# A transformer layer's down projection by seven products of half-size blocks

## The chip, the core and the metric

The kernel runs on one core of a Trainium2 chip. A core has a matrix engine (TensorE, PE in the rows; its weight loads are PEld), VectorE (DVE), ScalarE (ACT), GpSimd (POOL), and SyncE (SP), whose queue issues all the transfers between the chip's main memory and the on-chip memory SBUF. TensorE adds up its results in eight banks of a second memory, PSUM. The metric is the device time of one execution in microseconds (us). Every engine takes its instructions strictly in the order of its own queue and waits for the others by semaphores.

## The reference

One layer on 1024 tokens of width 1024: two mixers, merged and projected, then a SwiGLU network with 2816 hidden channels and a gated embedding. The change lies in the third line below and in what leads to and from it.

```python
x = x + merged @ w_out
hf = rms_norm(x, norm_ffn_g)
x = x + (jax.nn.silu(hf @ w_ffn_gate) * (hf @ w_ffn_up)) @ w_ffn_down
hp = rms_norm(x, norm_ple_g)
x = x + jax.nn.sigmoid(hp @ w_ple_gate) * (p @ w_ple_proj)
```

## The kernel before

Everything is held transposed: channels lie on the 128 partitions, the 1024 tokens on the free axis, in two halves of 512 (`hv(t, h)`). Each float32 operand is split into two parts of a shorter format: `split_to` lets ScalarE cast it to hi (line 1046) and VectorE subtract to lo (line 1047), `split_scaled` does it in lines 171 and 174. One product of blocks is then three matmuls of 128x128 by 128x512, hi by hi, hi by lo and lo by hi (`mm3`, lines 154 to 156).

**Gate and up** (lines 1156 to 1184) run over 22 values of f, one for each 128 hidden channels. This stage already computes the two pairs of half-size products by seven products instead of eight, each of 12 matmuls (`block`). For that, `ffn_weights(f + 1)`, called in the middle of f, forms four differences of the weights: two on GpSimd (lines 1132 and 1133) and two on VectorE (1134, which needs the result of 1133, and 1135). The blocks alternate between PSUM's tags z and m, three banks each; line 1161 copies the second block's bank (s1, the bank that line 1169 reads again) and VectorE adds the others (lines 1163, 1166, 1169, 1173, 1175, 1180). GpSimd also does lines 1176 and 1179 (twice). The hidden channels c11 and u4 (one for each half of the tokens) are stored in main memory, `hid` (line 1184), and SP fetches the weights of f + 2 in lines 1124 and 1126.

**The down projection** (lines 1241 to 1268) runs over two halves of the output channels and 22 values of f. In each of the 44 steps it loads half of the weights' tile (256 KB, line 1216) and one tile of hidden (512 KB, line 1219), splits both, and does 24 matmuls into eight banks: four blocks of output channels by two halves of tokens. The first two steps use buffers that exist before this stage. After 22 steps VectorE adds the eight banks to x1, the layer's x so far, which is loaded from `x1d` (line 1259), and `residual_norm` prepares the operands of the last stage. That last stage multiplies by `w_ple_gate`.

The order of TensorE's work is that of the program text (`manual_schedule`). On the other engines a scheduler of the language sets the order by its own estimates when the kernel is built; it may put an instruction far ahead of its place in the text if its inputs and its buffer are free.

Of the kernel before, what the change touches and what calls it, by code (L numbers as in the profile page):

```python
# [9 lines left out]
F32 = mybir.dt.float32  # L10
R = mybir.dt.float32r
# [3 lines left out]
ALU = mybir.AluOpType  # L15
# [4 lines left out]
P = 128  # L20
T = 1024
# [4 lines left out]
NFF = D_FF // P  # L26
HG_HEADS = 4
# [35 lines left out]
def layer(ctx, tc, xT, pT, wts, wf_in, consts, masks, outT):  # L63
# [37 lines left out]
    def wide(tag, dt, bufs=None):  # L101
        return wpool.tile([P, WIDE], dt, tag=tag, bufs=bufs, name=tag)
# [43 lines left out]
    def weight(u, ahead=2):  # L146
        for i in range(pos[u], min(pos[u] + ahead + 1, len(order))):
            if (order[i] < U_GATE) == (u < U_GATE):
                prep(order[i])
        return splits.pop(u)  # L150

    def mm3(ps, w, x, k, first, last):

        mm(ps, w[0], x[0], start=first, stop=False)  # L154
        mm(ps, w[0], x[1], start=False, stop=False)  # L155
        mm(ps, w[1], x[0], start=False, stop=last)  # L156
# [959 lines left out]
    hid = dram.tile([D_FF, T], F32, name="hid")  # L1116
    w6 = lambda: bp.tile([P, HALF], F32, tag="w6", name="w6")
    w7 = lambda: ap.tile([P, HALF], F32, tag="w7", bufs=4, name="w7")
# [36 lines left out]
    bp = astack.enter_context(tc.tile_pool(name="bp", bufs=8, reuse_waits="tile"))  # L1155
    for f in range(NFF):
# [26 lines left out]
        for h, s in ((0, c11), (1, u4)):  # L1183
            dma(hid[f * P:(f + 1) * P, h * HALF:(h + 1) * HALF], s)
# [5 lines left out]

    x1p = ctx.enter_context(tc.tile_pool(name="x1p", bufs=8, side="right", reuse_waits="tile"))
    dq = ctx.enter_context(tc.tile_pool(name="dq", bufs=4, reuse_waits="tile"))
    dp = ctx.enter_context(tc.tile_pool(name="dp", bufs=3, reuse_waits="tile"))
    hp = [[], []]
    x1 = []
    acc = const.tile([P, T], F32, tag="rb", name="acc")

    def residual_norm(j, h, t):
        hp[h].append(split_scaled(t, sm[:, S_PLE + j:S_PLE + j + 1], h))
        if j == 0:  # L1200
            act(hv(acc, h), t, AF.Square)
        else:
            sq = dp.tile([P, HALF], F32, tag="o", bufs=4, name="sq")
            act(sq, t, AF.Square)
            ptt(hv(acc, h), hv(acc, h), sq, ALU.add)  # L1205

    def down_operands(half, f):
        if half == 0 and f < 2:
            raw = hv(wide("raw", F32, 2)[:, 0:D], 0)
            hi = hv(wide("whi", R)[:, 0:D], 0)  # L1210
            lo = hv(wide("wlo", R)[:, 0:D], 0)
        else:
            raw = dp.tile([P, HALF], F32, tag="dr", name="dr")
            hi = dp.tile([P, HALF], R, tag="dhi", name="dhi")
            lo = dp.tile([P, HALF], R, tag="dlo", name="dlo")
        dma(raw, wts[U_DOWN + f][:, half * HALF:(half + 1) * HALF])
        w = split_to(raw, None, hi, lo)
        raw = wide("raw", F32, 2)[:, 0:D]
        dma(raw, hid[f * P:(f + 1) * P, :])
        return w, [split_scaled(hv(raw, h), None, h) for h in range(2)]  # L1220
# [15 lines left out]
    def down_order():  # L1236
        for half in range(2):
            for f in (range(NFF) if half == 0 else range(NFF - 1, -1, -1)):
                yield half, f

    todo = list(down_order())
    ready = [down_operands(*todo[i]) for i in range(2)]
    for n, (half, f) in enumerate(todo):
        w, a = ready.pop(0)
        first, last = n % NFF == 0, n % NFF == NFF - 1
        if first:
            banks = [[abank(), abank()], [zbank(), zbank()], [zbank(), mbank()], [mbank(), mbank()]]
        if n + 2 < len(todo):
            ready.append(down_operands(*todo[n + 2]))
        if n == NFF + 4:  # L1250
            ple_operands()
        for jj in range(4):
            s = slice(jj * P, (jj + 1) * P)
            for h in range(2):
                mm3(banks[jj][h], (w[0][:, s], w[1][:, s]), a[h], f, first, last)
        if first:
            for jj in range(4):
                t = x1p.tile([P, T], F32, tag="x1", name="x1")
                dma(t, x1d[(half * 4 + jj) * P:(half * 4 + jj + 1) * P, :])
                x1.append(t)  # L1260
        if last:
            for jj in range(4):
                for h in range(2):
                    t = hv(x1[half * 4 + jj], h)
                    tt(t, banks[jj][h], t, ALU.add)
            for jj in range(4):
                for h in range(2):
                    residual_norm(half * 4 + jj, h, hv(x1[half * 4 + jj], h))
# [10 lines left out]
    def gate_products(w, bank, h, ks):  # L1279
        for k in ks:  # L1280
            s = slice(k * P, (k + 1) * P)
            mm3(bank, (w[0][:, s], w[1][:, s]), hp[h][k], k, k == 0, k == KT - 1)
# [101 lines left out]
```

## Time and profile before

| | us |
|---|---|
| median of three runs | 1667.92 (1667.17 to 1668.07) |
| the profiled execution | 1666.99 |
| its span, first to last instruction | 1665.2 |
| gate and up, about | 883.6 to 1302.7 |
| down projection, about | 1302.7 to 1547.6 |

The profile is of one execution. Its views are a page with the busy shares, groups of instructions by line, a timeline, and tables by stretches of time. A row names the line of the kernel, the engine, the operation, what it writes and reads (buffer numbers left out), the shape, and in square brackets how long the engine was idle before it and whose work ended that.

### The profile page before, as it was taken

Reading aid. Unit: us, or ns where it says so; the run is one execution under the profiler, and the core shown is the slowest. Engines: PE = TensorE matmul, PEld = TensorE weight load, DVE = VectorE, ACT = ScalarE, POOL = GpSimd, SP = SyncE. Lnnn points to the kernel's source line nnn. Section 1 sums busy time; section 2 is a strip of 40 time slices with the busy share of each in tenths; the row PEclk is TensorE's granted clock in tenths of the full one; section 3 lists DMA queues with packets and bytes.
Section 4 is the critical chain, followed back from the end, with each engine's and each line's share of the span. In section 5 each row is a group of like instructions: output and inputs, shape, how many; then the busy total and the mean of one; then the engine's idle time right before and its main releaser. Section 6 shows DMA issues by size and latency. Waiting matters only on the chain. (4 is left out here: it accounts for less than half of the span.)

```text
span 1665.2 us, 21335 instructions
## 1 busy us (share of the span) xinstructions
PE 1639.5 (98%) x8218; PEld 1375.5 (83%) x8218; DVE 1041.2 (63%) x1466; ACT 634.4 (38%) x943; POOL 455.1 (27%) x364
## 2 busy tenths in 40 slices
PE   8999999999999999999999999999999999999998
PEld 6889889999797777778888888888888788788887
DVE  8357778755666676565677776666777442643542
ACT  7244655642423134551344333333333342543310
POOL 2342444531313021122234444344343000200300
PEclk9999999999999999999999999999999999999999
DMA  5323121236263632361433222222221663354020
GB/s 209 102 86 105 64 77 39 77 105 189 84 158 109 183 94 85 114 228 51 152 139 102 76 77 96 94 76 76 76 89 65 243 230 114 121 201 140 26 76 38
DMA packets 93685, 185.94 MB, mean 112 GB/s; under 512 B 11376, under 2 KB 40432, under 8 KB 93584
## 3 DMA queue, kind: packets, MB, share of 16 engines
q1 hardware_dynamic: 93584, 184.59, 33.9%
q8 instruction: 64, 1.05, 0.3%
q14 instruction: 37, 0.30, 0.1%
HBM read 130.95 MB, written 40.96 MB: 103 GB/s over the span
## 5 line engine op out<-in xcount | busy, mean ns | idle before, releaser
L154 PE MATMUL ps_z<-xhi,whi 128*128 128x512 f32 x630 | 255.1, 405 | 1.4 <-DVE w L1175 0.6
L155 PE MATMUL ps_z<-xlo,whi 128*128 128x512 f32 x630 | 246.5, 391 | 0.8 <-DVE xlo L174 0.5
L156 PE MATMUL ps_z<-xhi,wlo 128*128 128x512 f32 x630 | 246.0, 390 | 0.0
L154 PEld LDWEIGHTS ps_z<-xhi,whi 128*128 128x128 f32 x630 | 119.4, 190 | 23.5 <-DVE w L1175 1.1
L156 PEld LDWEIGHTS ps_z<-xhi,wlo 128*128 128x128 f32 x630 | 118.3, 188 | 24.8
L155 PEld LDWEIGHTS ps_z<-xlo,whi 128*128 128x128 f32 x630 | 118.8, 189 | 23.4 <-DVE xlo L174 2.0
L127 ACT CAST whi<-raw 128x1024 fp32r<-128x1024 f32 (+1 forms) x69 | 72.4, 1049 | 163.9 <-PE ps_z L155 126.6
L128 DVE TENSOR_TENSOR wlo<-raw,whi 128x1024 fp32r<-128x1024 f32 (+1 forms) x69 | 99.3, 1440 | 35.3 <-ACT whi L127 24.4
L174 DVE TENSOR_TENSOR xlo<-raw,xhi 128x512 fp32r<-128x512 f32 x88 | 58.7, 689 | 92.4 <-ACT xhi L171 82.1
L400 PE MATMUL ps_z<-whi,xhi 128*128 128x256 f32 (+1 forms) x384 | 112.8, 294 | 0.0
L401 PE MATMUL ps_z<-wlo,xhi 128*128 128x256 f32 (+1 forms) x384 | 108.7, 283 | 0.0
L402 PE MATMUL ps_z<-whi,xlo 128*128 128x256 f32 (+1 forms) x384 | 108.5, 283 | 0.0
L888 POOL TENSOR_SCALAR ph<-p 128x512 fp32r<-128x512 f32 (+3 forms) x96 | 53.5, 562 | 169.9 <-ACT p L884 169.5
L1179 POOL TENSOR_TENSOR w<-w,rb 128x512 f32<-128x512 f32 x44 | 62.8, 1428 | 114.1 <-ACT w L1178 114.1
L171 ACT ACTIVATE xhi<-raw 128x512 fp32r<-128x512 f32 x88 | 52.8, 626 | 104.6 <-PE ps_m L155 57.7
L889 DVE TENSOR_TENSOR pl<-p,ph 128x512 fp32r<-128x512 f32 (+3 forms) x96 | 55.9, 590 | 49.2 <-POOL ph L888 48.8
L1205 POOL TENSOR_TENSOR acc<-acc,sq 128x512 f32<-128x512 f32 x14 | 22.2, 1617 | 227.3 <-issue 116.6
L401 PEld LDWEIGHTS ps_z<-wlo,xhi 128*128 128x128 f32 x384 | 73.3, 191 | 0.7
L400 PEld LDWEIGHTS ps_z<-whi,xhi 128*128 128x128 f32 x384 | 73.4, 191 | 0.1
L402 PEld LDWEIGHTS ps_z<-whi,xlo 128*128 128x128 f32 x384 | 73.0, 190 | 0.0
L884 ACT ACTIVATE p<-ps_m 128x512 f32<-128x512 f32 (+3 forms) x96 | 46.2, 491 | 70.2 <-PE ps_m L880 46.9
L1134 DVE TENSOR_TENSOR rg<-ru,rg 128x512 f32<-128x512 f32 x22 | 36.7, 1667 | 55.4 <-POOL ru L1133 55.4
(465 smaller groups left out, 4380.8 us busy)
## 6 DMA issues: line engine op xcount, KB each, us to landing
raw<-wts SPq DMA_DIRECT2D x71, 512.0 KB
raw<-hid SPq DMA_DIRECT2D x44, 512.0 KB
rg<-wts SPq DMA_DIRECT2D x22, 512.0 KB
ru<-wts SPq DMA_DIRECT2D x22, 512.0 KB
hid<-w SPq DMA_DIRECT2D x44, 256.0 KB
dr<-wts SPq DMA_DIRECT2D x42, 256.0 KB
gd<-gst SPq DMA_DIRECT2D x24, 256.0 KB
g<-gd SPq DMA_DIRECT2D x24, 256.0 KB
```

The costliest lines, as they stand in the source:

```text
L127: nc.scalar.copy(hi, raw)
L128: tt(lo, raw, hi.bitcast(F32), ALU.subtract)
L154: mm(ps, w[0], x[0], start=first, stop=False)
L155: mm(ps, w[0], x[1], start=False, stop=False)
L156: mm(ps, w[1], x[0], start=False, stop=last)
L174: tt(lo, src, hi.bitcast(F32), ALU.subtract)
L400: mm(ps[:, off:off + n], xh[:, cs], hi, start=k == 0, stop=False)
L401: mm(ps[:, off:off + n], xh[:, cs], lo, start=False, stop=False)
L402: mm(ps[:, off:off + n], xl[:, cs], hi, start=False, stop=k == KT - 1)
L888: pts(ph[:, 0:n], p[:, 0:n], 1.0, 0.0, ALU.mult, ALU.add)
L889: tt(pl[:, 0:n], p[:, 0:n], fb(ph[:, 0:n]), ALU.subtract)
L1179: ptt(s, s, hv(rb, h), ALU.mult)
```

## The change

The down projection, too, is done by seven products of half-size blocks. The hidden channels are taken in 11 pairs of f (kp): the two tiles of a pair and the two halves of the tokens give four blocks, the pair's weights and the two halves of the output channels give four more. For each pair there are seven hidden operands (B11, B21, B22 as they are, T1 to T4 differences) and seven weight operands (three as they are, S1 to S4 sums). All of one product's 11 pairs are done before the next product begins, in 77 steps of 12 matmuls into four banks; a bank is added to the output blocks that contain its product (the lists in `products`), some while it goes on accumulating.

The sums are formed during gate and up: `down_sums` loads a quarter of a pair's weights into the tile sw, of which there is one, GpSimd does four operations 256 wide, and the result is stored to `sd`. `store_hidden` and the lines before it do the differences of the hidden channels on GpSimd and store the operands to `hb`. A step of the down projection loads two pieces of 256 KB into one tile (now four buffers) and splits them together. All eight x1 tiles are loaded early in the stage, and the first two gate products of the last stage are put in another order.

```diff
+NPAIR = NFF // 2
...
-    def mm3(ps, w, x, k, first, last):
-        mm(ps, w[0], x[0], start=first, stop=False)
-        mm(ps, w[0], x[1], start=False, stop=False)
-        mm(ps, w[1], x[0], start=False, stop=last)
+    def mm3(ps, w, x, k, first, last, more=False):
+        mm(ps, w[0], x[0], start=first, stop=False, skip_group_check=more)
+        mm(ps, w[0], x[1], start=False, stop=False, skip_group_check=more)
+        mm(ps, w[1], x[0], start=False, stop=last, skip_group_check=more)
...
-    hid = dram.tile([D_FF, T], F32, name="hid")
+    sd = dram.tile([NPAIR, P, 4 * HALF], F32, name="sd")
+    hb = dram.tile([7, NPAIR, P, HALF], F32, name="hb")
+    B11, B21, B22, T1, T2, T3, T4 = range(7)
+    S2, S3, S4, S1 = range(4)
     w6 = lambda: bp.tile([P, HALF], F32, tag="w6", name="w6")
+    def down_sums(kp, q):
+        t = bp.tile([P, 4, 256], F32, tag="sw", bufs=1, name="sw")
+        for i in range(2):
+            src = wts[U_DOWN + 2 * kp + i].rearrange("p (b c) -> p b c", b=2)
+            dma(t[:, 2 * i:2 * i + 2, :], src[:, :, q * 256:(q + 1) * 256])
+        ptt(t[:, 3], t[:, 1], t[:, 3], ALU.add)
+        ptt(t[:, 1], t[:, 0], t[:, 1], ALU.subtract)
+        ptt(t[:, 0], t[:, 3], t[:, 0], ALU.subtract)
+        ptt(t[:, 2], t[:, 2], t[:, 0], ALU.subtract)
+        dst = sd[kp].rearrange("p (b c) -> p b c", b=4)
+        dma(dst[:, :, q * 256:(q + 1) * 256], t)
+    def store_hidden(kp, even, b21, b22):
+        b11, b12, t1 = even
+        dma(hb[B21, kp], b21)
+        dma(hb[B22, kp], b22)
+        ptt(b12, b22, b12, ALU.subtract)
+        dma(hb[T3, kp], b12)
+        t2 = w6()
+        ptt(t2, b22, t1, ALU.subtract)
+        dma(hb[T2, kp], t2)
+        t4 = w6()
+        ptt(t4, b21, t2, ALU.subtract)
+        dma(hb[T4, kp], t4)
...
-    bp = astack.enter_context(tc.tile_pool(name="bp", bufs=8, reuse_waits="tile"))
+    bp = astack.enter_context(tc.tile_pool(name="bp", bufs=9, reuse_waits="tile"))
...
-        for h, s in ((0, c11), (1, u4)):
-            dma(hid[f * P:(f + 1) * P, h * HALF:(h + 1) * HALF], s)
+        down_sums(f // 2, f % 2)
+        if f % 2 == 0:
+            dma(hb[B11, f // 2], c11)
+            t1 = w6()
+            ptt(t1, u4, c11, ALU.subtract)
+            dma(hb[T1, f // 2], t1)
+            even = (c11, u4, t1)
+        else:
+            store_hidden(f // 2, even, c11, u4)
...
-    dp = ctx.enter_context(tc.tile_pool(name="dp", bufs=3, reuse_waits="tile"))
-    hp = [[], []]
+    dp = ctx.enter_context(tc.tile_pool(name="dp", bufs=4, reuse_waits="tile"))
...
-    def down_operands(half, f):
-        if half == 0 and f < 2:
-            raw = hv(wide("raw", F32, 2)[:, 0:D], 0)
-            hi = hv(wide("whi", R)[:, 0:D], 0)
-            lo = hv(wide("wlo", R)[:, 0:D], 0)
-        else:
-            raw = dp.tile([P, HALF], F32, tag="dr", name="dr")
-            hi = dp.tile([P, HALF], R, tag="dhi", name="dhi")
-            lo = dp.tile([P, HALF], R, tag="dlo", name="dlo")
-        dma(raw, wts[U_DOWN + f][:, half * HALF:(half + 1) * HALF])
-        w = split_to(raw, None, hi, lo)
-        raw = wide("raw", F32, 2)[:, 0:D]
-        dma(raw, hid[f * P:(f + 1) * P, :])
-        return w, [split_scaled(hv(raw, h), None, h) for h in range(2)]
+    lower = lambda kp, i, half: wts[U_DOWN + 2 * kp + i][:, half * HALF:(half + 1) * HALF]
+    summed = lambda kp, i: sd[kp][:, i * HALF:(i + 1) * HALF]
+    products = [
+        (lambda kp: lower(kp, 0, 0), B11, 0, True, [(0, 1), (1, 0), (1, 1)], []),
+        (lambda kp: summed(kp, S2), T2, 1, True, [(0, 1)], []),
+        (lambda kp: lower(kp, 1, 0), B21, 0, False, [(0, 0)], [(0, 0)]),
+        (lambda kp: summed(kp, S3), T3, 1, False, [(1, 1)], []),
+        (lambda kp: summed(kp, S1), T1, 0, True, [(1, 1)], [(1, 1)]),
+        (lambda kp: lower(kp, 1, 1), T4, 1, False, [(1, 0)], [(1, 0)]),
+        (lambda kp: summed(kp, S4), B22, 0, False, [(0, 1)], [(0, 1)]),
+    ]
+    todo = [(p, kp) for p in range(7) for kp in range(NPAIR)]
+    def down_operands(p, kp):
+        raw = dp.tile([P, D], F32, tag="dr", name="dr")
+        dma(hv(raw, 0), products[p][0](kp))
+        dma(hv(raw, 1), hb[products[p][1], kp])
+        return split_to(raw, None, wide("whi", R)[:, 0:D], wide("wlo", R)[:, 0:D])
...
-    def down_order():
-        for half in range(2):
-            for f in (range(NFF) if half == 0 else range(NFF - 1, -1, -1)):
-                yield half, f
-    todo = list(down_order())
     ready = [down_operands(*todo[i]) for i in range(2)]
-    for n, (half, f) in enumerate(todo):
-        w, a = ready.pop(0)
-        first, last = n % NFF == 0, n % NFF == NFF - 1
-        if first:
-            banks = [[abank(), abank()], [zbank(), zbank()], [zbank(), mbank()], [mbank(), mbank()]]
+    second = [abank(), abank(), mbank(), mbank()]
+    banks = [[zbank(), zbank(), zbank(), mbank()], second]
+    for n, (p, kp) in enumerate(todo):
+        hi, lo = ready.pop(0)
         if n + 2 < len(todo):
             ready.append(down_operands(*todo[n + 2]))
-        if n == NFF + 4:
+        elif n + 2 == len(todo):
+            prep(U_PG)
+        if n == 3:
+            for j in range(8):
+                t = x1p.tile([P, T], F32, tag="x1", name="x1")
+                dma(t, x1d[j * P:(j + 1) * P, :])
+                x1.append(t)
+        if n == 4 * NPAIR:
             ple_operands()
+        if n == 6 * NPAIR:
+            fetch(U_PG)
+            fetch(U_PG + 1)
+        _, _, g, begin, into, done = products[p]
         for jj in range(4):
             s = slice(jj * P, (jj + 1) * P)
-            for h in range(2):
-                mm3(banks[jj][h], (w[0][:, s], w[1][:, s]), a[h], f, first, last)
-        if first:
-            for jj in range(4):
-                t = x1p.tile([P, T], F32, tag="x1", name="x1")
-                dma(t, x1d[(half * 4 + jj) * P:(half * 4 + jj + 1) * P, :])
-                x1.append(t)
-        if last:
-            for jj in range(4):
-                for h in range(2):
-                    t = hv(x1[half * 4 + jj], h)
-                    tt(t, banks[jj][h], t, ALU.add)
-            for jj in range(4):
-                for h in range(2):
-                    residual_norm(half * 4 + jj, h, hv(x1[half * 4 + jj], h))
+            mm3(banks[g][jj], (hi[:, s], lo[:, s]), (hv(hi, 1), hv(lo, 1)), kp, begin and kp == 0,
+                kp == NPAIR - 1, not begin)
+        if kp == NPAIR - 1:
+            for fh, th in into:
+                for jj in range(4):
+                    t = hv(x1[fh * 4 + jj], th)
+                    tt(t, banks[g][jj], t, ALU.add)
+            for fh, th in done:
+                for jj in range(4):
+                    residual_norm(fh * 4 + jj, th, hv(x1[fh * 4 + jj], th))
...
     bps = [ple_project(0)]
     bgs = [[zbank(), zbank()], [zbank(), mbank()]]
-    w = weight(U_PG)
-    for ks in (range(4), range(4, KT)):
-        for h in range(2):
-            gate_products(w, bgs[0][h], h, ks)
-    w = weight(U_PG + 1)
-    gate_products(w, bgs[1][0], 0, range(KT))
+    w = [weight(U_PG), weight(U_PG + 1)]
+    late = (4, 5, 6, 7, 0, 1, 2, 3)
+    gate_products(w[0], bgs[0][0], 0)
+    gate_products(w[1], bgs[1][0], 0)
+    gate_products(w[0], bgs[0][1], 1, late)
     r8 = rms_stats(acc, mbank)
-    gate_products(w, bgs[1][1], 1, range(KT))
+    gate_products(w[1], bgs[1][1], 1, late)
```

What this does to the order is read from the built programs. The names in brackets are semaphores: DMAHW is a finished transfer, DVE, PE, Pool and Activation are engines. The lines of the changed kernel are about 33 higher: its 1132 to 1135 are the four operations of a sum, its 1165 and 1166 are the former 1132 and 1133, its 1209 and 1212 the former 1176 and 1179, its 1202 the former 1169; 1220, 1143, 1146 and 1149 are the new differences of hidden.

GpSimd, gate and up, before: a little over one f in the middle of the stage.

```order
L1176 TENSOR_TENSOR w_8971<-w_9001,w_8971 128x512 [waits DVE_49]
L1132 TENSOR_TENSOR ru<-ru 128x512 [waits DMAHW2_49,DVE_49]
L1133 TENSOR_TENSOR ru<-rg,ru 128x512 [waits DMAHW1_49,Pool_49]
L1179 TENSOR_TENSOR w_9139<-w_9139,rb 128x512 [waits DMAHW7_49,Activation_49]
L1179 TENSOR_TENSOR w_9141<-w_9141,rb 128x512 [waits DMAHW0_49,Activation_49]
L1176 TENSOR_TENSOR w_9110<-w_9140,w_9110 128x512 [waits DVE_49]
L1132 TENSOR_TENSOR ru<-ru 128x512 [waits DMAHW6_49,DVE_49]
L1133 TENSOR_TENSOR ru<-rg,ru 128x512 [waits DMAHW5_49,Pool_49]
```

Five operations stand in each f here, and those for the weights wait for their loads and for VectorE.

GpSimd, changed, the later part of an f with three sums in it, up to the next weights.

```order
L1212 TENSOR_TENSOR w_8916<-w_8916,rb 128x512 [waits DMAHW6_49,Activation_49]
L1209 TENSOR_TENSOR w_8885<-w_8915,w_8885 128x512 [waits DVE_49]
L1132 TENSOR_TENSOR sw<-sw 128x256 [waits DMAHW6_49,DMAHW7_49,DMAHW0_49,Pool_49]
L1133 TENSOR_TENSOR sw<-sw 128x256 [waits Pool_49]
L1134 TENSOR_TENSOR sw<-sw 128x256 [waits Pool_49]
L1135 TENSOR_TENSOR sw<-sw 128x256 [waits Pool_49]
L1220 TENSOR_TENSOR w_9030<-w_8916,w_8914 128x512 [waits DVE_49]
L1132 TENSOR_TENSOR sw<-sw 128x256 [waits DMAHW6_49,DMAHW7_49,DMAHW3_49,Pool_49]
L1133 TENSOR_TENSOR sw<-sw 128x256 [waits Pool_49]
L1134 TENSOR_TENSOR sw<-sw 128x256 [waits Pool_49]
L1135 TENSOR_TENSOR sw<-sw 128x256 [waits Pool_49]
L1165 TENSOR_TENSOR ru<-ru 128x512 [waits DVE_49]
```

Where two instructions stood between line 1179 and the next weights, two whole sums stand in addition. Each first operation of a sum (line 1132) waits for a transfer, and line 1165 stands behind it. All 22 sums come before the thirteenth 1165, 2 on average for each f.

SP, gate and up, before: the transfers of one f.

```order
L1184 DMA hid<-w_9139 128x512 [waits DMAHW4_49,DVE_49]
L1124 DMA rg<-wts 128x1024 [waits DMAHW6_49,DMAHW5_49,DVE_49]
L1126 DMA ru<-wts 128x1024 [waits DVE_49]
L1184 DMA hid<-w_9280 128x512 [waits DMAHW7_49,DVE_49]
L1184 DMA hid<-w_9278 128x512 [waits DMAHW0_49,DVE_49]
```

Weights and hidden channels alternate here, and nothing waits for GpSimd.

SP, changed, an odd f: from the store of a sum to the load of the next (lines 1137 and 1130).

```order
L1137 DMA sd<-sw 512x1x256 [waits DMAHW2_49,DMAHW4_49,DMAHW1_49,Pool_49]
L1142 DMA hb<-w_9065 128x512 [waits DMAHW5_49,DVE_49]
L1144 DMA hb<-w_8916 128x512 [waits Pool_49]
L1141 DMA hb<-w_9063 128x512 [waits DVE_49]
L1147 DMA hb<-w_9182 128x512 [waits Pool_49]
L1150 DMA hb<-w_9185 128x512 [waits Pool_49]
L1159 DMA ru<-wts 128x1024 [waits Activation_49]
L1130 DMA sw<-wts 128x2x256 [waits DMAHW4_49,DMAHW3_49]
L1130 DMA sw<-wts 128x2x256
```

The load of the next sum stands behind the five stores of hidden operands, the last of which waits for GpSimd's last difference, and behind a load of weights.

SP at the start of the down projection, before: the loads for the first steps (lines 1216 and 1219) among the last stores of hidden.

```order
L1216 DMA raw<-wts 128x512 [waits DMAHW6_49,DMAHW5_49,DVE_49]
L1219 DMA raw<-hid 128x1024 [waits DVE_49]
L1184 DMA hid<-w_10948 128x512 [waits DMAHW7_49,DVE_49]
L1184 DMA hid<-w_10946 128x512 [waits DMAHW0_49,DVE_49]
L1184 DMA hid<-w_11087 128x512 [waits DMAHW1_49,DVE_49]
L1216 DMA raw<-wts 128x512 [waits DMAHW5_49,DMAHW2_49,DVE_49]
L1184 DMA hid<-w_11085 128x512 [waits DMAHW3_49,DVE_49]
L1219 DMA raw<-hid 128x1024 [waits DMAHW6_49,DMAHW4_49,DVE_49]
L1219 DMA raw<-hid 128x1024 [waits DMAHW4_49,DVE_49]
L1219 DMA raw<-hid 128x1024 [waits DMAHW2_49,DVE_49]
L1219 DMA raw<-hid 128x1024 [waits DMAHW7_49,DMAHW5_49,DVE_49]
L1219 DMA raw<-hid 128x1024 [waits DMAHW6_49,DMAHW0_49,DVE_49]
```

The loads of the first step stand ahead of three of the last stores here, and those of the second step among and behind them.

SP, changed, at the same place: `dr` is the tile that a step loads.

```order
L1221 DMA hb<-w_11462 128x512 [waits DMAHW2_49,Pool_49]
L1142 DMA hb<-w_11497 128x512 [waits DMAHW3_49,DVE_49]
L1144 DMA hb<-w_11348 128x512 [waits DMAHW4_49,Pool_49]
L1147 DMA hb<-w_11590 128x512 [waits DMAHW5_49,Pool_49]
L1267 DMA dr<-wts 128x512 [waits DMAHW6_49,PE_49,Activation_49]
L1141 DMA hb<-w_11495 128x512 [waits DMAHW7_49,DVE_49]
L1150 DMA hb<-w_11593 128x512 [waits DMAHW0_49,Pool_49]
L1268 DMA dr<-hb 128x512 [waits DMAHW1_49]
L1267 DMA dr<-wts 128x512 [waits DMAHW2_49]
L1268 DMA dr<-hb 128x512 [waits DMAHW3_49]
L1267 DMA dr<-wts 128x512 [waits DMAHW4_49,PE_49]
L1268 DMA dr<-hb 128x512 [waits DMAHW5_49]
```

The hidden operand of the first step (line 1268) is now issued behind the last two stores of hidden. The eight loads of x1 (line 1297) follow after six steps' loads, in one row, where there were four and then one at a time.

## Rows read from the trace of the kernel before

**Rows 1.** The page, busy time of the engines: us, share of span, instructions.

```profile
PE 1639.5 (98%) x8218; PEld 1375.5 (83%) x8218; DVE 1041.2 (63%) x1466; ACT 634.4 (38%) x943; POOL 455.1 (27%) x364
```

**Rows 2.** Stretches: busy us (instructions) of each engine, granted clock, DMA share, GB/s.

```profile
883.60:1302.70 419.10, 418.38 (x1858) 346.72 (x1859) 296.42 (x362) 137.38 (x187) 171.83 (x107) 1.00 0.24 84
1302.00:1314.00 12.00, 9.11 (x39) 6.88 (x38) 8.57 (x14) 4.83 (x9) 2.54 (x2) 1.00 0.59 190
1318.00:1322.00 4.00, 4.00 (x19) 3.34 (x18) 1.29 (x2) 0.74 (x2) 0.00 (x0) 1.00 0.99 349
1326.00:1330.00 4.00, 4.00 (x19) 3.30 (x18) 1.60 (x3) 2.20 (x4) 0.00 (x0) 1.00 1.02 414
1400.00:1500.00 100.00, 98.48 (x434) 81.19 (x434) 50.51 (x71) 41.19 (x70) 9.38 (x6) 1.00 0.43 142
```

**Rows 3.** Timeline of GpSimd in one f: start, duration, instruction, idle before.

```profile
1065.19 1.67 POOL L1132 TENSOR_TENSOR ru<-ru 128x512 f32<-128x512 f32 x1 [6.36 <-DVE wlo L1047]
1066.94 1.29 POOL L1133 TENSOR_TENSOR ru<-rg,ru 128x512 f32<-128x512 f32 x1
1068.19 1.29 POOL L1179 TENSOR_TENSOR w<-w,rb 128x512 f32<-128x512 f32 x1
1074.10 1.56 POOL L1179 TENSOR_TENSOR w<-w,rb 128x512 f32<-128x512 f32 x1 [4.62 <-ACT w L1178]
1075.60 2.29 POOL L1176 TENSOR_TENSOR w<-w,w 128x512 f32<-128x512 f32 x1
1084.23 1.67 POOL L1132 TENSOR_TENSOR ru<-ru 128x512 f32<-128x512 f32 x1 [6.34 <-DVE wlo L1047]
```

**Rows 4.** Timeline of VectorE in the same f.

```profile
1068.26 1.77 DVE L1134 TENSOR_TENSOR rg<-ru,rg 128x512 f32<-128x512 f32 x1 [2.55 <-POOL ru L1133]
...
1070.55 0.68 DVE L1135 TENSOR_TENSOR rg<-rg 128x512 f32<-128x512 f32 x1
1071.15 0.68 DVE L1169 TENSOR_TENSOR w<-ps_z,w 128x512 f32<-128x512 f32 x1
...
1074.40 0.68 DVE L1175 TENSOR_TENSOR w<-ps_z,w 128x512 f32<-128x512 f32 x1
1075.01 1.73 DVE L1047 TENSOR_TENSOR sblo<-rg,sbhi 128x1024 fp32r<-128x1024 f32 x1
```

**Rows 5.** Groups by line: busy us, mean ns of one, idle us before.

```profile
L532 POOL TENSOR_TENSOR w<-Q,w 128x1024 f32<-128x1024 f32 x4 | 10.0, 2494 | 0.5 <-DVE el L530 0.5
...
L1133 POOL TENSOR_TENSOR ru<-rg,ru 128x512 f32<-128x512 f32 x15 | 19.3, 1289 | 1.2
...
L1047 DVE TENSOR_TENSOR salo<-ru,sahi 128x1024 fp32r<-128x1024 f32 x15 | 18.3, 1218 | 0.0
...
L1170 DVE TENSOR_TENSOR w<-w,rb 128x512 f32<-128x512 f32 x16 | 11.0, 688 | 0.0
```

**Rows 6.** Timeline of ScalarE: a block's copy, and two steps of the down projection.

```profile
1077.36 0.59 ACT L1159 COPY w<-ps_z 128x512 f32<-128x512 f32 x1 [1.45 <-PE ps_z L156]
...
1365.56 0.63 ACT L171 ACTIVATE xhi<-raw 128x512 fp32r<-128x512 f32 x1 [3.61 <-PE ps_m L155]
...
1371.00 0.63 ACT L171 ACTIVATE xhi<-raw 128x512 fp32r<-128x512 f32 x1 [3.61 <-PE ps_m L155]
```

**Rows 7.** Timeline of SP, ScalarE, VectorE: transfers issued, first uses, last addition.

```profile
866.12 0.33 SPq L1126 DMA_DIRECT2D ru<-wts  x1
...
869.43 0.62 ACT L1046 CAST whi<-ru 128x512 fp32r<-128x512 f32 x1 [1.42 <-DMA ru<-wts]
...
1291.10 0.32 SPq L1219 DMA_DIRECT2D raw<-hid  x1
...
1295.76 0.63 ACT L171 ACTIVATE xhi<-raw 128x512 fp32r<-128x512 f32 x1 [5.64 <-DMA raw<-hid]
...
1661.61 0.69 DVE L1290 TENSOR_TENSOR o<-o,x 128x512 f32<-128x512 f32 x1
```

More of the change, by code (lines that the diff above doesn't have):

```diff
@@ L1192, in layer @@
     dq = ctx.enter_context(tc.tile_pool(name="dq", bufs=4, reuse_waits="tile"))
-    dp = ctx.enter_context(tc.tile_pool(name="dp", bufs=3, reuse_waits="tile"))
-    hp = [[], []]
+    dp = ctx.enter_context(tc.tile_pool(name="dp", bufs=4, reuse_waits="tile"))
+    hp = [[None] * KT, [None] * KT]
     x1 = []
     acc = const.tile([P, T], F32, tag="rb", name="acc")
+    started = set()
     def residual_norm(j, h, t):
-        hp[h].append(split_scaled(t, sm[:, S_PLE + j:S_PLE + j + 1], h))
-        if j == 0:
+        hp[h][j] = split_scaled(t, sm[:, S_PLE + j:S_PLE + j + 1], h)
+        if h not in started:
+            started.add(h)
             act(hv(acc, h), t, AF.Square)
@@ L1277, in ple_project, with gate_products @@
         return bp
-    def gate_products(w, bank, h, ks):
-        for k in ks:
+    def gate_products(w, bank, h, ks=range(KT)):
+        for i, k in enumerate(ks):
             s = slice(k * P, (k + 1) * P)
-            mm3(bank, (w[0][:, s], w[1][:, s]), hp[h][k], k, k == 0, k == KT - 1)
+            mm3(bank, (w[0][:, s], w[1][:, s]), hp[h][k], k, i == 0, i == KT - 1)
     def ple_finish(j, bg, bp):
```

## The prediction

> **What bounds the kernel now.** Read the busy shares of the page first: the span is 1665.2 us and TensorE is busy for 1639.5 of it at full granted clock [rows 1, 2]. Then the stages: from 883.6 to 1302.7 us (gate and up, 22 values of f) TensorE is busy for 418.4 of 419.1 us, and in the down projection it loses 2.9 us of the 12 between 1302 and 1314 and 1.5 us between 1400 and 1500 [rows 2]. So what counts is the number of matmuls, and whether the other queues keep up. Third, GpSimd and VectorE inside one f: GpSimd's first product of f comes every 19.04 us (1065.19 to 1084.23), and in between it does five 512-wide operations and is idle twice, 4.6 and 6.3 us [rows 3]. Those two gaps are where the new sums would have to go. VectorE's rows of the same f show what the gaps are worth: L1134, with both inputs in SBUF, takes 1.77 us where it starts beside GpSimd's L1179 and L1135 of the same size takes 0.68 alone; L1176 on GpSimd takes 2.29 beside the split sblo, against 1.29 of L1133, of its size [rows 3, 4]. L1175, with one input in PSUM, is not lengthened beside L1179. So a two-SBUF-input operation of VectorE and an operation of GpSimd exclude each other.
>
> **Removed.** 44 steps of 24 matmuls become 77 steps of 12: 1056 to 924, 132 fewer. A step of 24 takes 5.44 us (split at 1365.56, next 1371.00, released by PE [rows 6]), so 226.7 ns each and 29.9 us less. A new step lasts 2.72 us; it needs one 1024-wide cast and one 1024-wide subtraction (1.22 us, [rows 5]), which fit, and 512 KB per 2.72 us, 193 GB/s, where the trace has moved 414 in a stretch [rows 2]. A raw tile (four of them) is refilled once its split is done and wanted four steps on, some 8.5 us, against landings of 3.3 to 4.7 us [rows 7]. I cost the steady steps at nothing beyond TensorE; without that cover they would be rival E.
>
> **Added to gate and up.** 22 calls of down_sums with four 256-wide operations, and 44 differences 512 wide. One of 512 takes 1.29 and one of 1024 takes 2.49 [rows 5], so on that line 256 takes 0.70: 88 x 0.70 = 62 us, and 44 x 1.29 = 57 us. GpSimd has 10.9 idle us per f. But the order of the program puts all 22 sums between the weights of f = 1 and of f = 12, two per f, not one (first pieces of order in the change).
> The Trainium skill, "GPSIMD Engine Reference" (3.1, Elementwise), gives 4497 ns for an addition of 2048 elements a partition; an estimate in proportion is 0.56 us for 256, which no run here shows yet. By that the sums would take 12 us less of GpSimd's time, about 1 us less in each of 11 periods.
>
> What decides is the order. There is one buffer for a sum (bufs=1): load 512 KB, four operations, store 512 KB, and only then the next load. A landing of 512 KB took 3.3 us (issued 866.12, used 869.43) and 4.7 us in a fuller queue (1291.10 to 1295.76). The store of 256 KB after the last addition (1661.61 + 0.69) ends the span, 2.9 us; 512 KB at some 340 GB/s adds 0.7, so 3.6 [rows 7]. With 0.3 for the issues a turnaround T is 7.2 us; from below 6.6 (store as quick as the load), from above 9.5 (the fuller queue both ways).
> The Trainium skill, "DMA: Bandwidth & Descriptors" (Anatomy of one DMA), has a fixed 2.0 us plus the bytes over 436 GB/s: by estimate 3.2 us for 512 KB, with which the 3.3 us agrees and the 4.7 us does not. By it T would be 6.7 and the sum below some 8 us smaller.
> GpSimd is in order, so a sum at the head of its queue that waits for its load holds up L1132/L1133 of the next weights (L1165/L1166 in the changed kernel). These release VectorE's L1134, behind which L1169 stands, the last reader of the bank that the next f's first block takes. In the trace L1169 ends at 1071.83 [rows 4]; that first block ends just before its copy at 1077.36 [rows 6] and its 12 matmuls take 2.7, so it starts at 1074.6. GpSimd may then be 2.7 us late in each f and no more: its own period may be 21.7 us.
> Now GpSimd's queue, by kind of period (names of the changed kernel, whose L1132 to L1135 are a sum):
> - Two and three quarters of a sum (four periods): L1165, the other three operations of sum A, L1166, L1212 with VectorE's operations between: 1.7 + 3 x 0.7 + 2 x 1.3 + 2 x 0.6 = 7.6. Wait T, sum B with three VectorE operations in between (0.6 + 1.2 + 0.6): 5.2. Wait T, sum C: 2.8. Together 30 us with T = 7.2. With no exclusion and T = 6.6: 24.8.
> - One and a quarter (four periods): sum D starts after T, 7.2; its four operations with L1212 and two splits between (2.8 + 1.3 + 2.3) end at 13.6, L1209 and the VectorE product behind it at 15.5, the three differences with 0.6 and 1.2 of VectorE between at 21. SP issues the next load behind the store of T4, which waits for the last difference (SP's pieces of order): about 1 us of issues, 3.3 landing, one operation: 26 us. From below 21.7.
> - Two sums (three periods): about 25, from below 21.
> Sum 4 x 30 + 4 x 26 + 3 x 25 = 299 us for 11 periods that take 11 x 19.04 = 209.5 now: +89; from below 249, +39; with T = 9.5 some 345, +135. The walk charges each exclusion in full; I take +70, between the low end and the walk and nearer to the walk, since every pair of two-SBUF operations in [rows 3, 4] that meets shows the full exclusion. The later ten f have no sums: 8.5 us of VectorE (three 1.22, seven 0.69) and 7.6 or 10.3 of GpSimd in 19.04 us fit, cost 0. The stores of hidden cost nothing: SP has nothing urgent behind them then, weights being fetched one f ahead.
>
> **Start of the down projection.** The first input of step 0 is now fetched behind the store of the last T4 (last pieces of order): before, the first two steps used the old buffers and were fetched before gate and up ended. From the end of TensorE's last block: two VectorE operations and GpSimd's last difference 4.5 us, landing 2.9, cast and subtraction 2.3: about 9.5 us idle in place of 2.9: +6. Then eight x1 tiles (4.2 MB) stand in SP's queue ahead of step 6, behind 3 MB for steps 0 to 5, which are in at about 15 us. At 349 to 414 GB/s [rows 2] x1 takes 10 to 12 us, step 6 with its landing and split is ready at 29 to 31 and wanted at 9.5 + 6 x 2.72 = 25.8: +4.
> **Ends of products.** After product 0 VectorE has twelve additions of 0.6 and one split ahead of the split of step 13: that is ready 7.2 + 1.2 + 1.2 = 9.6 us after the product's end and wanted at 5.4: +4; the four later ends with four additions and four gain splits +0.5 each: +2. The 1.5 us lost at the old half's end go. Tail and last layer: no change.
>
> **Sum.** -29.9 + 70 + 6 + 4 + 6 - 1.5 = +54.6 on the profiled execution's 1667.0 us (1665.2 and 1.8 around it); the median is 0.9 above it, so 1722.5: **slower**, 1722 us.
>
> **Rivals.**
> A. The forecast: GpSimd's queue waits for the transfers of the sums. With all else as above its own range is 1692 (+39) to 1742 (+89).
> B. Only the exclusion counts, transfers hidden: per f 8.5 + 6.45 + 2.6 + 5.6 = 23.1 us of exclusive time against 19.04, or 21.6 with the 0.60 us at which VectorE's 512-wide operations follow each other (1070.55 to 1071.15 [rows 4]): +28 to +45, 1681 to 1698. For it: the lengthened operations [rows 3, 4]. Against: the single buffer.
> C. Loaded turnarounds of 9.5 us: +135, 1787. For it: the 4.7 us landing, and 1 KB runs, which no row prices. Against: 84 GB/s in gate and up [rows 2].
> D. The sums fit: the period of three sums stays under 21.7 us if T is under 5.1, since 11.5 + 2T; then TensorE sets the pace as before and 1668 - 30 + 14.5 = 1652, faster. For it: 10.9 idle us per f. Against: no 512 KB landing here takes under 3.3 us, and T holds two.
> E. The down projection isn't fed: 3.0 us per step instead of 2.72, +22 on A: 1744. Against: the loads and splits above.
>
> **How the numbers follow.** A 0.55, B 0.15, C 0.15, D 0.08, E 0.07. The range 1683 to 1768 holds A, E, most of B and half of C and leaves out D: about 0.8. A run tells 0.2% (3 us) from no change: faster 0.08 (D), same 0.03 (between D and B), slower 0.89.
>
> **What would show it.** A right: in f = 1 to 11 L1165 on GpSimd comes every 22 to 30 us, the first operation of a sum (L1132 there) waits for the DMA of sw, TensorE waits in that stretch for L1202, and from f = 12 on the period is 19.04 again. Down projection: 77 steps of 2.72 us, a gap of 9 to 10 us before the first, a smaller one at steps 6 and 13. It is wrong if the period stays under 21.7 us with the sums in it, and more so if TensorE's stretch from f = 1 to 11 stays at 209 us.

## The result: 1753.4 us, slower by 5.1%

The changed kernel takes 1753.41 us (median of four runs, 1751.07 to 1753.79) against 1667.99 us before; the ratio is 1.0509, 95% interval 1.0491 to 1.0527. The forecast said slower, 1722 us, with a range of 1683 to 1768: the sign and the place were right, the loss is 85 us where 54.6 were forecast.

The busy shares and the granted clock of the page, to set against [rows 1]:

```profile
PE 1638.8 (94%) x8086; PEld 1368.2 (78%) x8086; DVE 1095.8 (63%) x1431; ACT 637.5 (36%) x888; POOL 607.7 (35%) x496
...
PEclk9999999999999999999998888988999979999999
```

TensorE does 132 matmuls less and is busy as long as before: some of its time passes at a lower clock, in the stretch of gate and up and where the down projection starts. The stretches of the changed kernel (columns as in [rows 2]):

```profile
879.28:1400.42 521.14, 445.70 (x1873) 363.37 (x1871) 326.54 (x361) 137.13 (x186) 321.19 (x239) 0.92 0.36 126
894.70:1202.60 307.90, 238.57 (x960) 192.23 (x958) 166.44 (x178) 67.61 (x92) 198.32 (x165) 0.88 0.42 143
...
1400.40:1412.00 11.60, 0.34 (x2) 0.17 (x1) 6.83 (x7) 1.04 (x1) 4.52 (x3) 0.64 0.70 229
```

The same two parts of the kernel before, gate and up from its first matmul and all that follows:

```profile
879.88:1302.92 423.04, 421.93 (x1873) 349.34 (x1872) 300.16 (x365) 140.09 (x190) 173.37 (x108) 1.00 0.25 86
1302.92:1665.20 362.28, 352.59 (x1561) 290.43 (x1559) 159.54 (x226) 115.58 (x190) 26.35 (x17) 1.00 0.39 131
```

Gate and up went from 423.0 to 521.1 us, +98.1. The rest, up to the end of the span, went from 362.3 to 351.3 (1751.7 - 1400.4), -11.0. All of the first loss lies in the 11 periods that hold the sums: 307.9 us for 11 f, where [rows 3] has 19.04 us for one. GpSimd in one of these periods (start, duration, instruction, idle before and who ended it):

```profile
1029.82 1.26 POOL L1165 TENSOR_TENSOR ru<-ru 128x512 f32<-128x512 f32 x1
1031.16 1.26 POOL L1166 TENSOR_TENSOR ru<-rg,ru 128x512 f32<-128x512 f32 x1
1032.38 1.26 POOL L1212 TENSOR_TENSOR w<-w,rb 128x512 f32<-128x512 f32 x1
1037.26 0.84 POOL L1132 TENSOR_TENSOR sw<-sw 128x256 f32<-128x256 f32 x1 [3.62 <-DMA sw<-wts]
1038.26 2.09 POOL L1212 TENSOR_TENSOR w<-w,rb 128x512 f32<-128x512 f32 x1 [0.15 <-ACT w L1211]
...
1048.77 2.16 POOL L1149 TENSOR_TENSOR w<-w,w 128x512 f32<-128x512 f32 x1
1056.67 0.72 POOL L1132 TENSOR_TENSOR sw<-sw 128x256 f32<-128x256 f32 x1 [5.74 <-DMA sw<-wts]
1057.35 1.26 POOL L1165 TENSOR_TENSOR ru<-ru 128x512 f32<-128x512 f32 x1
```

Twice a sum's first operation waits for its transfer, the second time with line 1165, the next weights, behind it. The waits in all these periods (engine and line, for whom; us in total, times, longest):

```profile
DVE rg L1167 <- POOL ru L1166: 113.4, 12, 13.7
...
POOL sw L1132 <- DMA sw<-wts: 89.0, 22, 6.5
...
PE ps_z L156 <- DVE w L1199: 39.1, 5, 8.9
...
PE ps_m L156 <- DVE w L1199: 34.5, 5, 8.5
```

All 22 sums wait, VectorE waits for the weights' difference on GpSimd, and TensorE for VectorE. TensorE waits 75 of the 98 us, and its matmuls take the other 23 longer, at a lower clock (445.7 us busy against 421.9, with as many records). Its rows at one of these waits:

```profile
941.42 0.39 PE L158 MATMUL ps_z<-xo,wlo 128*128 128x512 f32 x1
950.29 0.79 PE L156 MATMUL ps_m<-xo,whi 128*128 128x512 f32 x1 [8.48 <-DVE w L1199]
950.88 0.63 PE L157 MATMUL ps_m<-xo,whi 128*128 128x512 f32 x1
951.30 0.63 PE L158 MATMUL ps_m<-xo,wlo 128*128 128x512 f32 x1
...
956.42 0.42 PE L158 MATMUL ps_z<-xo,salo 128*128 128x512 f32 x1
956.68 0.40 PE L156 MATMUL ps_z<-xo,sahi 128*128 128x512 f32 x1
956.91 0.40 PE L157 MATMUL ps_z<-xo,sahi 128*128 128x512 f32 x1
```

For 6 us after the wait one starts every 0.43 us, then every 0.23 again. The granted clock is 0.50 from 951 to 956 us: the lower of its two levels, 1.2 of 2.4 GHz.

### The profile page after: what moved, and what is told of

Its sections match the earlier page's. It is cut to its first block, busy times and chain, and to the rows that moved or that the text cites. A ratio compares the mean times of both kernels' runs of the same rounds, so it can differ in the third digit from the quotient of the medians.

```text
span 1751.7 us, 21446 instructions
## 1 busy us (share of the span) xinstructions
PE 1638.8 (94%) x8086; PEld 1368.2 (78%) x8086; DVE 1095.8 (63%) x1431; ACT 637.5 (36%) x888; POOL 607.7 (35%) x496
## 4 chain that ended last, share of the span: by engine, by line
PE 67%; POOL 10%; DMA 8%; issue 6%; DVE 6%; ACT 2%; SPq 1%; POOLq 0%; DVEq 0%; ACTq 0%
PE ps_z L156 11%; PE ps_z L157 11%; PE ps_z L158 11%; DMA sw<-wts 4%; PE ps_m L156 3%; PE ps_m L158 3%; PE ps_m L157 3%; PE ps_z L402 3%; PE ps_z L403 3%; PE ps_z L404 3%; DMA sd<-sw 2%; POOL sw L1133 1%; PE ps_m L488 1%; POOL sw L1134 1%; POOL sw L1135 1%
## 5 line engine op out<-in xcount | busy, mean ns | idle before, releaser
L1049 DVE TENSOR_TENSOR wlo<-dr,whi 128x1024 fp32r<-128x1024 f32 x77 | 100.4, 1309 | 83.8 <-ACT whi L1048 83.7
L1048 ACT CAST whi<-dr 128x1024 fp32r<-128x1024 f32 x77 | 81.0, 1052 | 128.5 <-PE ps_m L158 103.9
L156 PE MATMUL ps_z<-xo,whi 128*128 128x512 f32 x132 | 56.3, 426 | 39.1 <-DVE w L1199 39.1
L156 PE MATMUL ps_m<-xo,whi 128*128 128x512 f32 x132 | 56.4, 427 | 34.5 <-DVE w L1199 34.5
L1211 ACT ACTIVATE w<-w 128x512 f32<-128x512 f32 x44 | 27.9, 633 | 155.1 <-DVE w L1207 82.9
```

Of the source, the lines that this page charges most:

```text
L156: mm(ps, w[0], x[0], start=first, stop=False, skip_group_check=more)
L1048: nc.scalar.copy(hi, src)
L1049: tt(lo, src, hi.bitcast(F32), ALU.subtract)
```

## The experiments

In the table, "gate and up" is from the stage's first matmul to its last, "rest" from there to the end of the span.

| | time, us | gate and up | rest |
|---|---|---|---|
| before | 1668.0 | 423 | 362 |
| changed | 1753.4 | 521 | 351 |
| e1 one sum in each f, text order | 1708.0 | 470 | 356 |
| e2 no sums | 1653.9 | 423 | 352 |
| e3 two sums in a row in 11 f | 1784.4 | 548 | 353 |
| e4 the same, no transfers | 1716.5 | 482 | 353 |
| e5 the changed order, no transfers | 1688.7 | 458 | 351 |
| e6 one sum in each f, in the gap | 1655.4 | 423 | 353 |
| e7 and the first two steps early | 1651.2 | 423 | 346 |
| e8 and x1 one at a time | 1645.0 | 423 | 342 |
| e9 and the last pair on VectorE | 1643.3 | 423 | 339 |

### Where the loss of gate and up comes from: e2 and e5

e2 drops the sums:

```diff
-        down_sums(f // 2, f % 2)
...
-    summed = lambda kp, i: sd[kp][:, i * HALF:(i + 1) * HALF]
+    summed = lambda kp, i: wts[U_DOWN + 2 * kp + i % 2][:, i // 2 * HALF:(i // 2 + 1) * HALF]
```

> Leaves out the 22 sums (their loads, operations and stores); the down projection reads original weights of the same size in their place, so all its loads stand. The 44 differences of hidden and their stores stay. All theories: gate and up goes back to 419 us if the differences cost nothing (every period 19.04), and the rest of the kernel is as in the changed one, so 1753.4 - 98 = 1655 us. If the differences cost something of their own (theory B: 8.5 + 6.45 + 2.6 = 17.6 us of exclusive time fit, so no), periods over 19.04 appear in the odd f.

Measured 1653.85 us (ratio 0.9925, 0.9909 to 0.994). Gate and up is back at 423 us, so the 44 differences and 77 stores cost nothing and the sums are the whole 98 us.

e5 keeps GpSimd's queue as it was and takes the transfers away. `sum_steps` gives one operation of a sum at a time, and a list says how many follow each other operation of GpSimd:

```diff
-        down_sums(f // 2, f % 2)
...
+                if t is None:
+                    t = bp.tile([P, 4, 256], F32, tag="sw", bufs=1, name="sw")
+                    for i in range(2):
...
+                yield gtt(t[:, 3], t[:, 1], t[:, 3], ALU.add)
...
+    def dtt(*a):
+        gtt(*a)
+        for _ in range(next(behind, 0)):
+            next(steps)
```

> GpSimd's queue as in the changed kernel, operation for operation (its order there is written out by hand here; one pair of instructions in the first f changes places), and TensorE's, ScalarE's and VectorE's queues the same; but the sums' tile is loaded once and never stored, so that no sum waits for a transfer (the down projection reads original weights instead of sums). A: the waits for transfers were the whole loss: the period of f = 1 to 11 falls from 28.0 us to 19.04 to 20, gate and up from 516 to 419 to 430 us, the time to 1655 to 1667 us. B: the operations' exclusion was the loss and the waits hid behind it: 21.6 to 23.1 us, 447 to 464 us, 1682 to 1700 us. The run with two sums in a row in each f and no transfers had 24.3 us, so something between is possible: then both count, the transfers for the part that goes away.

Measured 1688.68 us in one run, gate and up 457.5 us: between the two. So the transfers' turnaround is worth 64 us (521.1 - 457.5) and the operations alone, in this order, 34 us. Rival B, priced at +28 to +45 by itself, is real; it is not the larger part. GpSimd is busy for 207 of the 245 us of the 11 periods in this run; at 0.72 and 1.26 us each, the shortest in the changed kernel, the same operations would take 159, so much of the 34 us is probably their lengthening; how much of it is their order wasn't separated. In that run TensorE's waits are short (same columns):

```profile
PE ps_z L156 <- DVE w L1211: 10.7, 5, 2.4
PE ps_m L156 <- DVE w L1211: 8.3, 5, 2.2
```

### The same two sums in a row, with and without transfers: e3 and e4

```diff
-        down_sums(f // 2, f % 2)
+        for q in range(2 if f < NPAIR else 0):
+            down_sums(f, q)
```

> Text order as in the first run, but two whole sums in each of the first 11 f, one right behind the other, and none after. A: the second sum waits a whole turnaround of 7 us behind the first, and the period is 24 to 27 us in the first 11 f (gate and up 475 to 505 us), 19.04 after. B: 21.6 to 23.1 us, gate and up 447 to 464 us. TensorE's clock falls after each wait in both.

> As the run before, with the same operations in the same places, but the sums' tile is loaded once and never stored, so that no sum waits for a transfer (the down projection reads original weights instead of sums). A: the period is that of the engines alone, under 21.7 us and so 19.04 to 20; gate and up 419 to 430 us. B: as before, 21.6 to 23.1 us and 447 to 464 us. The difference to the run before is the price of the transfers in the queue's order.

Single runs, 1784.4 and 1716.5 us; gate and up 548 and 482 us. The periods are 30.3 us (897.36 to 1230.20 for 11) and 24.3 us: both theories had them too low, probably in part because the text order has a delay of its own, which e1 shows. The difference, 65 us for 22 sums, is the price of the transfers once more, as in e5.

### One sum in each f, in two places: e1 and e6

e1 puts GpSimd's queue in the order of the text:

```diff
-    order_pe = tc.manual_schedule(engines={mybir.EngineType.PE})
+    order_pe = tc.manual_schedule(engines={mybir.EngineType.PE, mybir.EngineType.Pool})
```

> GpSimd takes its instructions in the order of the program text in this stage, so that one sum stands in each of the 22 f, behind the two operations of line 1212 and ahead of the differences; every other queue but SP's is the same as in the changed kernel. Theory A (a sum at the head of GpSimd's queue waits for the store and the load of the single buffer): with 19 us from one sum to the next the turnaround of 7.2 us is over before the sum is reached, no first operation of a sum waits for a transfer, the period of f is 19.04 to 19.6 us throughout, gate and up takes 419 to 432 us instead of 516, TensorE's clock stays at 1.00 there, and the time is 1753.4 - 85 to 98 = 1655 to 1668 us. Theory B (GpSimd's and VectorE's operations exclude each other, transfers are hidden): the same 62 us of sums and 57 us of differences are still to be done, now over 22 f; 20.4 us of exclusive time per f in 19.04 leave +30 us in gate and up, 1684 us or more, and the period is 20.4 in every f. Theory C (TensorE's clock, which falls after each wait, makes the loss): it says what A says, since there are no waits.

Measured 1707.98 us (ratio 1.0242, 1.0225 to 1.0259), a miss for A: no sum waits for its load now, but gate and up still loses 47 us. The periods alternate between 23.3 and 19.8 us, which is not B's 20.4 in every f either. GpSimd in one f of this run, and then the wait of TensorE that follows:

```profile
1045.47 1.29 POOL L1166 TENSOR_TENSOR ru<-rg,ru 128x512 f32<-128x512 f32 x1
1052.62 2.21 POOL L1209 TENSOR_TENSOR w<-w,w 128x512 f32<-128x512 f32 x1 [5.87 <-DVE w L1208]
1054.79 2.53 POOL L1212 TENSOR_TENSOR w<-w,rb 128x512 f32<-128x512 f32 x2
1057.29 0.73 POOL L1132 TENSOR_TENSOR sw<-sw 128x256 f32<-128x256 f32 x1
...
1065.71 1.29 POOL L1149 TENSOR_TENSOR w<-w,w 128x512 f32<-128x512 f32 x1
1066.96 1.29 POOL L1165 TENSOR_TENSOR ru<-ru 128x512 f32<-128x512 f32 x1
```

```profile
1070.97 0.79 PE L156 MATMUL ps_m<-xo,whi 128*128 128x512 f32 x1 [2.80 <-DVE w L1199]
```

The queue's head is now line 1209, which waits 5.9 us for VectorE with the two products of line 1212 behind it (ScalarE had finished the first one's input at 1044.9, the second's at 1051.5); the sum and the differences come after and push the next weights back. So the trace shows the same fault with another instruction. Line 1209's place wasn't tested by itself: the next run moves both it and the sum.

e6 moves the sum between the two products, into the gap of 4.6 us of [rows 3], and line 1209 behind them:

```diff
-        ptt(p5, u2, p5, ALU.add)
         for s, h in ((c11, 0), (u4, 1)):
             act(s, s, AF.Silu)
             ptt(s, s, hv(rb, h), ALU.mult)
+            if h == 0:
+                down_sums(f // 2, f % 2)
+        ptt(p5, u2, p5, ALU.add)
...
-        down_sums(f // 2, f % 2)
```

> Text order on GpSimd again and one sum in each of the 22 f, but the order within f is the one that a schedule without sums has (weights, the two products of line 1212, then line 1209), and the sum stands between the two products, where GpSimd was idle for 4.6 us in each f before the change. A: no sum waits for a transfer, and none stands ahead of the weights or of line 1209, so the period is 19.04 in all f, gate and up 419 to 425 us, TensorE's clock 1.00, and 1654 to 1660 us, as without sums. B: 20.4 us of exclusive time per f in 19.04: gate and up 440 to 449 us, 1675 to 1684 us.

Measured 1655.43 us (ratio 0.9935, 0.992 to 0.9949), gate and up 423 us, as without sums. One odd f of GpSimd, from weights to weights (its 1211 and 1214 are 1212 and 1209):

```profile
1065.31 1.68 POOL L1165 TENSOR_TENSOR ru<-ru 128x512 f32<-128x512 f32 x1 [0.63 <-DVE wlo L1049]
1067.06 1.29 POOL L1166 TENSOR_TENSOR ru<-rg,ru 128x512 f32<-128x512 f32 x1
1068.31 1.29 POOL L1211 TENSOR_TENSOR w<-w,rb 128x512 f32<-128x512 f32 x1
1069.56 1.19 POOL L1132 TENSOR_TENSOR sw<-sw 128x256 f32<-128x256 f32 x1
1070.83 1.12 POOL L1133 TENSOR_TENSOR sw<-sw 128x256 f32<-128x256 f32 x1
1072.03 0.74 POOL L1134 TENSOR_TENSOR sw<-sw 128x256 f32<-128x256 f32 x1
1072.86 1.22 POOL L1135 TENSOR_TENSOR sw<-sw 128x256 f32<-128x256 f32 x1
1074.22 2.09 POOL L1211 TENSOR_TENSOR w<-w,rb 128x512 f32<-128x512 f32 x1
1076.28 2.26 POOL L1214 TENSOR_TENSOR w<-w,w 128x512 f32<-128x512 f32 x1
1079.35 1.29 POOL L1143 TENSOR_TENSOR w<-w,w 128x512 f32<-128x512 f32 x1 [0.81 <-DVE w L1217]
...
1085.20 1.68 POOL L1165 TENSOR_TENSOR ru<-ru 128x512 f32<-128x512 f32 x1 [0.63 <-DMA ru<-wts]
```

The sum takes 4.5 us, no operation of it waits, and GpSimd, busy for 352 of the 423 us, holds up TensorE nowhere, which waits 1.1 us in the whole stage. Operations are lengthened here too (line 1133 takes 1.12 us, line 1132 alone 0.72 in the changed kernel), and B's 20.4 us of exclusive time per f was too much. The Trainium skill, "SBUF — State Buffer" (Who interferes with whom), says that a VectorE instruction with two SBUF inputs contends with a GpSimd instruction that reads SBUF, over a pair of ports that one of them locks for itself; the lengthened rows agree with it, and the unchanged 423 us show that it costs nothing while neither engine sets the pace.

### The start of the down projection: e7, e8, e9

The changed kernel at the start of that stage and at the seventh step:

```profile
1400.19 0.39 PE L158 MATMUL ps_m<-xo,wlo 128*128 128x512 f32 x1
1411.83 0.79 PE L156 MATMUL ps_z<-whi 128*128 128x512 f32 x1 [11.26 <-ACT whi L1048]
1413.09 0.80 PE L157 MATMUL ps_z<-wlo,whi 128*128 128x512 f32 x1 [0.47 <-DVE wlo L1049]
...
1433.65 0.49 PE L156 MATMUL ps_z<-whi 128*128 128x512 f32 x1 [2.21 <-ACT whi L1048]
1434.91 0.80 PE L157 MATMUL ps_z<-wlo,whi 128*128 128x512 f32 x1 [0.77 <-DVE wlo L1049]
```

e7 adds to e6:

```diff
-        raw = dp.tile([P, D], F32, tag="dr", name="dr")
+        if (p, kp) < (0, 2):
+            raw = wide("raw", F32, 2)[:, 0:D]
+        else:
+            raw = dp.tile([P, D], F32, tag="dr", name="dr")
```

> As the run before, with the operands of the first two steps of the down projection loaded into the tiles that are there before this stage, so that their loads need not wait for the end of gate and up. If the first load, issued behind the last store of hidden, sets the gap at the start (11.3 us without work, then matmuls at half the clock for 5 us), the two steps fill 5.4 us of it, the rest of it shrinks to 4 to 6 us, the clock falls less, and the time is 6 to 9 us under that of the run before. If the splits or the last of TensorE's own results set it, no change.

Measured 1651.23 us (0.991, 0.9894 to 0.9927), 4.2 us less by the medians and 6.0 between the profiled executions (1656.36 and 1650.38): the direction held, the size came out at the low end of the forecast or under it. The wait only moves to the third step and shrinks from 11.1 to 7.0 us, and the clock falls there as well.

e8 adds:

```diff
-        if n == 3:
-            for j in range(8):
-                t = x1p.tile([P, T], F32, tag="x1", name="x1")
-                dma(t, x1d[j * P:(j + 1) * P, :])
-                x1.append(t)
+        if 2 <= n < 10:
+            t = x1p.tile([P, T], F32, tag="x1", name="x1")
+            dma(t, x1d[(n - 2) * P:(n - 1) * P, :])
+            x1.append(t)
```

> As the run before it (sum in the gap, first two steps early), with the eight x1 tiles loaded one in each of steps 2 to 9 instead of all in a row behind the loads of six steps. If the row of x1 loads in SP's queue makes the wait at the seventh step or so (2.6 + 0.8 us without work there, then some 5 us at a lower clock), the wait goes: 4 to 6 us less, 1645 to 1647 us. If the bytes are the limit (4.2 MB of x1 and 0.5 MB per step, at about 400 GB/s, for 10 steps), the wait is only spread out and the time is the same within 1 us.

Measured 1644.95 us (0.9871, 0.9854 to 0.9887), 6.3 us less. TensorE's waits for the first cast of a step, in e7 and then in e8 (columns as above):

```profile
PE ps_z L156 <- ACT whi L1048: 9.6, 2, 7.0
PE ps_z L156 <- ACT whi L1048: 6.7, 1, 6.7
```

Only the one at the third step is left: the row of x1 loads made the wait at the seventh, not the bytes.

e9 adds:

```diff
         b11, b12, t1 = even
+        ptt = tt if kp == NPAIR - 1 else nc.gpsimd.tensor_tensor
```

> As e8_x1_one_per_step, with the three differences of the last pair on VectorE, which is idle there, so that the last stores, and the loads queued behind them on SP, are issued about 2.5 us earlier. If the stores set the start of the third step's load, the wait of 7.0 us at the third step falls to about 4.5 us and the time by 2 to 4 us more, to some 1642 us. If the buffers (free only when TensorE has ended) or the landings set it, no change.

Measured 1643.26 us (0.9858, 0.9843 to 0.9872), 1.7 us less. TensorE's largest wait in this stage:

```profile
1312.36 0.80 PE L156 MATMUL ps_z<-whi 128*128 128x512 f32 x1 [4.27 <-ACT whi L1048]
```

It was 6.7 us in e8, so the stores do stand ahead of the loads. The part behind gate and up got 2.7 us shorter between the two profiled executions, about as much as the wait; the whole time fell by less there, since gate and up started 1.4 us later in the second (879.2 against 877.9), ahead of what this run changes. e9 is the fastest kernel here: 24 us under the one before, of the 29.9 us that the matmuls are worth.

## Why the prediction was right in kind and 31 us short

- **The mechanism held.** A sum at the head of GpSimd's queue waits for its transfer, 89.0 us in 22 waits, with the weights behind it, and the chain of work that ended last holds no matmul in the 11 periods. By the starts of line 1165, the periods with two and three quarters of a sum took 29.8 to 30.0 us, those with one and a quarter 27.4 to 27.9, those with two 21.4 (the first), 29.2 and 27.2; none is over 19.4 from f = 12 on.
- **The step that failed is the choice after the walk.** The walk through the queue gave 299 us, +89; measured 307.9 against 208.0 us (+99.9 by GpSimd's rows, +98.1 for the stage). I took +70, towards a low end in which the exclusion vanished. That choice is 19 of the 31 us: by the walk alone the forecast would have been 1742 us, the upper end of A. Another 9 are the walk's own, and the down projection is the rest. The reason given for leaving the walk, that it charges each exclusion in full, is not borne out: the four periods with the most sums took the 30 us of the walk, and without transfers (e5) the operations still cost 34 us. The two prices don't simply add either: e5 takes away 89.0 us of waits, and gate and up gets 64 us shorter, so a part of the operations' time lay hidden in the waits.
- **The walk's own 9 us** (308 instead of 299) lie in the shorter periods: 6.5 in the four with one and a quarter sums, 26 us on paper, and 2.8 in the three with two, 25 on paper. The sum behind the store of T4 is loaded right after a weights' load. The last difference ends at 1050.93, the load is issued at 1051.85 and used at 1056.67: 0.9 us of issues and 4.8 for the landing, where I had one and 3.3.
- **The turnaround**, taken as 7.2 us (6.6 to 9.5), was 7.5 where nothing else was queued. In SP's rows a store issued at 1064.04 ends at 1067.13, when the next load is issued, and line 1132 uses that at 1071.57.

```profile
1064.04 0.56 SPq L1137 DMA_DIRECT2D sd<-sw  x1
1067.13 1.20 SPq L1130 DMA_DIRECT2D sw<-wts  x2
```

  The rule of the Trainium skill, "DMA: Bandwidth & Descriptors" (Anatomy of one DMA), is fitted there to transfers that GpSimd issues, and SyncE issues these; my estimate of 6.7 us by it comes out low. So does the estimate of 0.56 us after the Trainium skill, "GPSIMD Engine Reference" (3.1, Elementwise): the shortest of the 88 operations of the sums takes 0.72, and 0.70 was taken.
- **The down projection** gained 11.0 us where 15.4 were forecast. Steps last 2.72 us, as worked out (casts on ScalarE):

```profile
1461.99 1.05 ACT L1048 CAST whi<-dr 128x1024 fp32r<-128x1024 f32 x1 [3.96 <-PE ps_m L158]
1464.71 1.05 ACT L1048 CAST whi<-dr 128x1024 fp32r<-128x1024 f32 x1 [1.67 <-PE ps_m L158]
```

  The first wait was 11.7 us instead of 9.5, that at the seventh step 3.0 instead of 4, those at the ends of products 2.0 instead of 6. What the sum lacked is TensorE's clock, which runs at half after the first two waits (granted 0.56 from 1412 to 1418): the twelve matmuls of the first step take 5.8 us (1411.83 to 1417.65), 0.5 of it waiting, instead of 2.7, and those at the seventh step 6.1 (0.8 of it waiting). With 0.7 more in the eighth the clock cost some 6 us, and the waits, together some 3 us shorter than forecast, hid half of that by luck. These terms make up 3 of the 4.4 us; the rest isn't accounted for.
- **The rivals.** B alone was priced at 1681 to 1698 us, and e5, which has the operations without the transfers, gives 1688.7. D, sums that fit at 1652 us, is not what the change does. The same 22 sums do fit at another place (e6, 1655.4), without D's condition, a shorter turnaround: each has a whole f for it, and none waits. C and E did not happen: the turnaround was 7.5 us and not 9.5, a step 2.72 and not 3.0.

## What to carry to other kernels

In an in-order queue the place of an instruction that waits is worth more than its work: the same 22 sums cost 98, 47 or 0 us, by their place in the queue: what waits ahead of them, and what they keep waiting. A buffer that is loaded, used and stored in turn needs its whole turnaround between two uses, so space such uses out and put them into a gap that the trace shows; and if a walk through the queue gives a number, forecast that number. Before a stage with small steps, see that its first loads don't stand behind the last stores, and that no row of large loads stands ahead of steps that come sooner.

## What the runs showed of the hardware

TensorE's granted clock fell to its lower level (1.2 of 2.4 GHz) in or right after every wait of 3.0 us and more in these traces, from gate and up on, and the matmuls behind such a wait came every 0.43 us instead of 0.23 for some 3 to 7 us, longer where another wait followed. Shorter waits don't settle it: in e5 it fell after one of 2.2 us (at 1075.8) and stayed at 1.00 after one of 2.4 (at 1008.4), and the waits of together 2.9 us between 1302 and 1314 in the kernel before, one of them 2.2, left it at 1.00 [rows 2]. In gate and up of the changed kernel the lower clock took 23 us of TensorE's time (521.1 - 423.0 - 75), which GpSimd's pace covered: in the 11 periods no matmul stands in the chain that ended last. In e1 that chain does hold some matmuls, and TensorE's waits are only 29 of the 47 us; what the clock would be worth there by itself wasn't tried.
